# Transposed probabilities of the first two token tiles in another buffer of an encoder kernel

## The chip, the cores and the metric

The kernel runs on one core of one Trainium2 chip. The metric is the device time of one execution in microseconds (us), as the median of several runs. The core has five engines with a queue of instructions each: TensorE (PE, with the weight loads shown apart as PEld), VectorE (DVE), ScalarE (ACT), GpSimd (POOL) and SyncE (SP), whose queue issues most of the transfers (DMA). An engine takes its instructions in the order of its queue; semaphores make it wait for the others.

## The reference

A hybrid encoder trunk of one layer on 1024 tokens with 1024 channels. Three residual sub-layers, each as `x <- LayerNorm(alpha * x + f(x))`: a token mixer (mLSTM heads beside neighbourhood attention), cross-attention from every token into 256 memory tokens, and a gated ConvFFN. The change lies at the seam between the first two. The attention and the sums around it:

```python
def memory_xattn(x, mem, w_q, w_kv, w_o, b_o):
    q = (x @ w_q).reshape(b, t, XA_HEADS, XA_DIM).astype(jnp.float32)
    ...
    s = jnp.einsum('bthd,bmhd->bhtm', q, k) * (XA_DIM ** -0.5)
    p = jax.nn.softmax(s, axis=-1)
    o = jnp.einsum('bhtm,bmhd->bthd', p, v).reshape(b, t, d).astype(x.dtype)
    return o @ w_o + b_o

h = layer_norm(DN_ALPHA * h + hybrid_mixer(...), ln1_w[l], ln1_b[l])
h = layer_norm(DN_ALPHA * h + memory_xattn(h, mem, ...), ln2_w[l], ln2_b[l])
h = layer_norm(DN_ALPHA * h + conv_ffn(h, ...), ln3_w[l], ln3_b[l])
```

## The kernel before, in words

Tokens are worked on in eight tiles of 128. Products are made in half precision with every operand split in a high and a low part, so that one product is three matmuls (`mm3`, lines 223 to 226: high x high on L224, high x low on L225, low x high on L226). These lines are shared by all stages; a row of the profile is told apart by its tiles.

**First norm.** The second half of the mixer's output product runs over the tiles in the order `todo = [0, 2, 1, 3, 4, 6, 5, 7]` (L1313). After each tile `after1` normalizes it (`ln_tile`), multiplies it with `ln1_w` on VectorE (L1305) and adds `ln1_b` on GpSimd (L1306). The two vectors lie in the buffers with the tags `vec0` and `vec1`, the bias `b_xo` in `vec2`. These three buffers are used again and again through the kernel.

**Cross-attention.** Key and value products are folded beforehand with the query and output weights, so that a tile needs two stages:

- `to_hT` (L1266) splits the normalized tile and has SyncE's queue transpose both parts (two DMA transposes, L1271) into `h1T`, of which there are two buffers. `scores(n)` makes 48 matmuls in two halves (`S<-kq,h1T`), takes maxima (L1392), exponentials (L1396), reciprocal sums (L1399), and splits the probabilities into `Ps` (ScalarE L203, VectorE L204).
- `to_PT(n)` has SyncE's queue transpose both parts of `Ps` (two DMA transposes, L1411) into a `vec` buffer: tile n in `vec0` or `vec1` by turns, the last in `vec2`. `out_d(n)` makes 48 matmuls with it (`S<-whi,vec`), adds the residual on VectorE (L1422), takes the second norm and stores the tile.

The loop around them does `scores(n + 1)`, `to_PT(n)`, `to_hT(n + 2)`, `out_d(n - 1)` for each n. `to_B` (L1325) follows `out_d` with a lag of one tile: TensorE transposes the normalized tile; an even tile is kept, an odd one makes the token sums T1 to T4 with its even partner, split in two parts on L1358 and L1359. T2 and T4 lie in the buffer X1h, T1 and T3 in X1l; both buffers are of 4096 float32 a partition and held, until then, the mixer's first half (read by the matmuls `fill`). The sums are operands of the ConvFFN's up-projection, whose weight units `Units.prep` prepares (GpSimd differences from L1521 on, splits on L203 and L204).

**What sets the order.** The program is written in the order above, but line 1927 opens the framework with `schedule_with_timeline_sim=True`: the order of each engine's queue is settled when the kernel is built, from a simulated timeline, with the order of the program as priority. A tile that is allocated in a buffer waits for all readers of the tile that held the buffer before (`reuse_waits="tile"`, L66 to L69). `issue_after` puts single instructions behind others by hand.

Of the kernel before, what the change touches and what calls it, by code (L numbers as in the profile page):

```python
# [8 lines left out]
F32 = mybir.dt.float32  # L9
# [8 lines left out]
D = 1024  # L18
# [38 lines left out]
def encoder(ctx, tc, I, out):  # L57
    nc = tc.nc
    V, A, G, T, S = nc.vector, nc.scalar, nc.gpsimd, nc.tensor, nc.sync
# [7 lines left out]
    vecs = ctx.enter_context(tc.tile_pool(name="vecs", bufs=1, reuse_waits="tile"))  # L67
    wp = ctx.enter_context(tc.tile_pool(name="weights", bufs=1, reuse_waits="tile"))
    xp = ctx.enter_context(tc.tile_pool(name="acts", bufs=1, reuse_waits="tile"))  # L69
# [15 lines left out]
    def tbank():  # L85
        return pp.tile([128, 512], F32, name="tp", tag="tp", bufs=2).rearrange("p (k t) -> p k t", k=4)
# [194 lines left out]
    with ExitStack() as ca:  # L281

        yml = None
        with ExitStack() as cm:
# [258 lines left out]
            with ExitStack() as c2:  # L543
# [12 lines left out]
                with ExitStack() as c1:  # L556
# [162 lines left out]
                T24, T13 = (xp.tile([128, 4096], F32, name="T" + x_, tag=x_).bitcast(F16).rearrange(  # L719
                    "p (n k t) -> p n k t", n=4, k=4) for x_ in ("X1h", "X1l"))  # L720
# [513 lines left out]
    with ExitStack() as cb_:  # L1234
# [3 lines left out]
        f16 = lambda t: t.bitcast(F16)  # L1238

        def evict_wb(q, dst, src, wb, i):  # L1240

            w, b = wb[:, i:i + 1], wb[:, 8 + i:9 + i]
            if q == 0 or i < 6:
                A.activation(dst, src, AF.Identity, scale=w, bias=b)
            else:
                V.tensor_scalar(dst, src, w, b, op0=OP.mult, op1=OP.add)
# [34 lines left out]
        with ExitStack() as cB:  # L1281
# [21 lines left out]
            def after1(tt, r):  # L1303
# [5 lines left out]
                if tt == todo[4]:  # L1309
# [6 lines left out]

        Bh = f16(xp.tile([128, 4096], F32, name="Bh", tag="X2h")).rearrange("p (n q k t) -> p n q k t", n=2, q=2, k=4)
        B1s = xp.tile([128, 4096], F32, name="Bf", tag="X2l").rearrange("p (i q k t) -> p i q k t", i=4, q=2, k=4)
        T24, T13 = (f16(xp.tile([128, 4096], F32, name="T" + t, tag=t)).rearrange("p (n k t) -> p n k t", n=4, k=4)
                    for t in ("X1h", "X1l"))  # L1320
        Bop = {"B11": (Bh[:, 0, 0], Bh[:, 1, 0]), "B21": (Bh[:, 0, 1], Bh[:, 1, 1]),
               "T1": (T13[:, 0], T13[:, 1]), "T3": (T13[:, 2], T13[:, 3]),
               "T2": (T24[:, 0], T24[:, 1]), "T4": (T24[:, 2], T24[:, 3])}

        def to_B(r, tt):  # L1325

            o = slice(tt // 2 * 128, tt // 2 * 128 + 128)
            pts = []
            for q in range(2):
                pt = tbank()  # L1330
                for k in range(4):
                    T.transpose(pt[:, k, :], r[:, (4 * q + k) * 128:(4 * q + k + 1) * 128], ident)
                pts.append(pt)
            B1 = B1s[:, tt // 2]
            spare = lambda i: vecs.tile([128, D], F32, name=f"spare{i}", tag=f"vec{i}")
            if tt % 2:
                if tt == todo[-1]:
                    r = spare(1)
                dst = [r[:, i * 512:i * 512 + 512].rearrange("p (k t) -> p k t", k=4) for i in range(2)]
            else:  # L1340
                dst = [B1[:, q] for q in range(2)]
            for q in range(2):
                for k in range(4):
                    i = 4 * q + k
                    evict_wb(q, dst[q][:, k], pts[q][:, k], wb2, i)
            if tt % 2 == 0:
                for q in range(2):
                    A.activation(Bh[:, 0, q, :, o], B1[:, q], AF.Copy)
                    V.tensor_tensor(Bh[:, 1, q, :, o], B1[:, q], Bh[:, 0, q, :, o], OP.subtract)
                return  # L1350
            e12, e22 = dst
            t12, t34 = ((spare(2 * i) if tt == todo[-1] else
                         wp.tile([128, WP], F32, name="wraw", tag="wraw", bufs=2)[:, :1024]).rearrange(
                "p (i k t) -> p i k t", i=2, k=4) for i in range(2))
            T1, T2, T3, T4 = t12[:, 0], t12[:, 1], t34[:, 0], t34[:, 1]
            def pair(n, src):
                h, l = (t[:, :, o] for t in Bop[n])
                A.activation(h, src, AF.Copy)  # L1358
                (G if n in ("B22", "T3") else V).tensor_tensor(l, src, h, OP.subtract)  # L1359

            V.tensor_tensor(T1, e12, B1[:, 0], OP.subtract)
            V.tensor_tensor(T2, e22, T1, OP.subtract)
            pair("T2", T2)
            pair("T1", T1)
            V.tensor_tensor(T3, e22, e12, OP.subtract)
            pair("B22", e22)
            pair("T3", T3)
            V.tensor_tensor(T4, B1[:, 1], T2, OP.subtract)
            pair("T4", T4)
# [11 lines left out]
        def scores(ck, n):  # L1381
# [21 lines left out]
                    split16(hl[:, 0, o], hl[:, 1, o], P[:, o], mn[:, 4 + h:5 + h])  # L1403
            return hl

        def to_PT(hl, n):
            i = 2 if n == NT - 1 else n % 2
            t = f16(vecs.tile([128, D], F32, name=f"vec{i}", tag=f"vec{i}")).rearrange(
                "p (n k t) -> p n k t", n=2, k=8)
            for i in range(2):  # L1410
                S.dma_start_transpose(t[:, i], hl[:, i])  # L1411
            probs[n] = t

        def out_d(n, lag=1):

            r, t, tt = rs.pop(n), probs.pop(n), todo[n]
            for ch in range(2):
                ps = bank("S2")
                c = slice(ch * 512, ch * 512 + 512)
                for k in range(8):  # L1420
                    mm3(ps, t[:, 0, k], t[:, 1, k], Vo[0][k][:, c], Vo[1][k][:, c], k == 0, k == 7)
                V.scalar_tensor_tensor(r[:, c], r[:, c], alx, ps, op0=OP.mult, op1=OP.add)  # L1422
                yield
            holds.append(ln_tile(r, None, None, small, hold=holds[-1] if holds else None, late=n == NT - 1, eps=epx))
            stores.append(S.dma_start(h2_d[tt * 128:(tt + 1) * 128, :], r))
            rq.append((r, tt))
            if len(rq) > lag:
                to_B(*rq.pop(0))
            yield
# [5 lines left out]
        for n in range(NT - 1):  # L1435
            Pn = scores(ck, n + 1)
            to_PT(P, n)
            P = Pn
            if n + 2 < NT:
                to_hT(ck, n + 2, rs[n + 2])  # L1440
                G.tensor_tensor(rs[n + 2], rs[n + 2], bxo, OP.add)
            if 0 < n < NT - 2:
                run(out_d(n - 1))
        to_PT(P, NT - 1)
        cC.close()

# [109 lines left out]
        next(o6)  # L1556
        next(prep0)
        to_B(*rq.pop(0))
        run(o6)
        run(prep0)  # L1560
# [7 lines left out]
        prep1 = units.prep(1, True)  # L1568
        next(prep1)
        to_B(*rq.pop(0))  # L1570

        with rtx:
# [201 lines left out]
        with ExitStack() as cF:  # L1774
# [13 lines left out]
            for j in range(1, 5):  # L1788
                for tt in range(NT):
# [3 lines left out]
                    if tt in (0, 4) and j < 4:  # L1793
                        f = 4 * j + 4 + tt // 2
# [29 lines left out]
            for tt in range(NT):  # L1824
# [10 lines left out]
                n = 256 if last else 512  # L1835
# [5 lines left out]
                for i in range(2 if last else 1):  # L1841
                    c = slice(i * 512, i * 512 + 512) if last else slice(0, D)
# [88 lines left out]
```

## Time and profile before

| what | us |
|---|---|
| median of 3 runs | 1515.85 (1513.14 to 1516.48) |
| profiled execution, own time | 1512.6 |
| its span, first to last instruction | 1510.5 |
| TensorE busy | 1444.8 (96%) |
| VectorE busy | 1038.1 (69%) |
| ScalarE busy | 824.9 (55%) |
| GpSimd busy | 575.0 (38%) |
| mean granted TensorE clock | 0.988 of full speed |

The profile is of one execution, by the hardware profiler. Times in its rows are from the start of the span, durations in us or, in groups, ns. A row of the timeline reads: start, duration, engine, line of the kernel, operation, tile written <- tiles read, shapes, how many; in square brackets the time that the engine stood idle before, and what it waited for. `SPq` is SyncE's queue of transfers. Matmuls are pipelined, and their ends are modelled: two of them that start 0.22 us apart are each shown with 0.38 us.

### The profile page before, as it was taken

To read this page: it belongs to the slowest core of one execution; us is meant where nothing else is said; L and a number is where in the kernel's file an instruction comes from. 1 tells how busy PE (TensorE), PEld (TensorE's weight loads), DVE (VectorE), ACT (ScalarE), POOL (GpSimd) and SP (SyncE) were. 2 spreads that over 40 slices of the span, in tenths; PEclk is the share of its full clock that TensorE was granted. 3 is DMA by queue.
4 is the path that set the end of the run, shared out by engine and by line. 5 is a ranking of instruction groups with operands and counts; after the bars stand their busy time and mean duration, and the time that the engine had idled before them with its cause. 6 is when DMAs were issued, how large, how long until landed. Compare 5 with 4: busy or idle time off the path is not lost. (4 is left out here: it accounts for less than half of the span.)

```text
span 1510.5 us, 21655 instructions
## 1 busy us (share of the span) xinstructions
PE 1444.8 (96%) x8060; PEld 867.4 (57%) x8060; DVE 1038.1 (69%) x1945; ACT 824.9 (55%) x1393; POOL 575.0 (38%) x453
## 2 busy tenths in 40 slices
PE   8999999999999898997999889999999999999998
PEld 6998776456766787863444434444444444444444
DVE  7867866546677678588455769887787789707424
ACT  5766565655544566424444768777777767503000
POOL 5442357303325765055111464434443420300543
PEclk9999999999999999998999989999999999999999
DMA  8846653325545634743332242223322436713121
GB/s 303 322 159 213 196 187 125 89 53 148 159 119 161 209 119 135 257 126 62 81 77 82 88 153 112 112 112 126 112 112 113 166 112 225 278 41 98 48 79 56
DMA packets 116383, 208.61 MB, mean 138 GB/s; under 512 B 40627, under 2 KB 69555, under 8 KB 112950
## 3 DMA queue, kind: packets, MB, share of 16 engines
q1 hardware_dynamic: 115984, 206.47, 41.3%
q8 instruction: 63, 1.03, 0.3%
q0 software_dynamic: 144, 0.49, 0.2%
q14 instruction: 42, 0.34, 0.1%
q10 hardware_dynamic: 150, 0.27, 0.0%
HBM read 154.15 MB, written 45.15 MB: 132 GB/s over the span
## 5 line engine op out<-in xcount | busy, mean ns | idle before, releaser
L1521 POOL TENSOR_TENSOR wraw<-ur 128x512 f32<-128x512 f32 x22 | 45.7, 2076 | 206.0 <-issue 191.1
L225 PE MATMUL dn<-wlo,yp 128*128 128x512 f16 (+1 forms) x284 | 105.1, 370 | 0.0
L224 PE MATMUL dn<-whi,yp 128*128 128x512 f16 (+1 forms) x284 | 104.9, 370 | 0.0
L226 PE MATMUL dn<-whi,yp 128*128 128x512 f16 (+1 forms) x284 | 104.4, 370 | 0.0
L1609 DVE SCALAR_TENSOR_TENSOR cbuf<-C,wdw,cbuf 128x1024 f32<-128x1024 f32 x44 | 69.6, 1583 | 35.1 <-ACT cbuf L1608 34.9
L226 PEld LDWEIGHTS <-wlo 128*128 128x128 f16 x540 | 52.8, 98 | 57.2 <-DVE wlo L204 1.9
L225 PEld LDWEIGHTS <-whi 128*128 128x128 f16 x540 | 52.8, 98 | 56.0 <-issue 3.2
L224 PEld LDWEIGHTS <-whi 128*128 128x128 f16 x540 | 52.9, 98 | 53.5 <-ACT whi L203 0.6
L242 POOL TENSOR_TENSOR lnrs<-lnrs,mhalf 128x1 f32<-128x1 f32 x32 | 26.0, 812 | 145.9 <-DVE lnrs L241 140.2
L204 DVE SCALAR_TENSOR_TENSOR wlo<-wraw,us,whi 128x1024 f16<-128x1024 f32 (+1 forms) x48 | 62.7, 1323 | 18.7 <-ACT whi L203 18.7
L1610 DVE SCALAR_TENSOR_TENSOR cbuf<-C,wdw,cbuf 128x1024 f32<-128x1024 f32 x44 | 70.2, 1596 | 0.7
L252 ACT ACTIVATE r<-r,lnrs 128x1024 f32<-128x1024 f32 x19 | 23.5, 1239 | 72.3 <-DVE lnrs L251 72.2
L203 ACT ACTIVATE whi<-wraw,us 128x1024 f16<-128x1024 f32 (+1 forms) x48 | 51.2, 1103 | 15.7 <-DVE us L176 14.8
L225 PEld LDWEIGHTS <-yp 128*128 128x128 f16 x370 | 36.2, 98 | 39.9
L224 PEld LDWEIGHTS <-yp 128*128 128x128 f16 x370 | 36.2, 98 | 39.9
L226 PEld LDWEIGHTS <-yp 128*128 128x128 f16 x370 | 36.2, 98 | 39.7
L1608 ACT ACTIVATE cbuf<-C,bdw,wdw 128x1024 f32<-128x1024 f32 x44 | 54.2, 1233 | 8.8 <-DVE C L1646 8.2
L224 PE MATMUL S<-whi,vec 128*128 128x512 f16 x128 | 49.5, 387 | 9.2 <-DMA vec<-Ps 9.2
L224 PE MATMUL tk<-whi,Bo 128*128 128x256 f16 (+1 forms) x192 | 53.3, 277 | 1.6 <-DVE stage L204 1.6
L225 PE MATMUL tk<-wlo,Bo 128*128 128x256 f16 (+1 forms) x192 | 53.4, 278 | 0.0
L226 PE MATMUL tk<-whi,Bo 128*128 128x256 f16 (+1 forms) x192 | 53.3, 278 | 0.0
L225 PE MATMUL tk<-wlo,Be 128*128 128x256 f16 (+1 forms) x192 | 52.4, 274 | 0.9 <-DVE wlo L204 0.9
(520 smaller groups left out, 4898.0 us busy)
## 6 DMA issues: line engine op xcount, KB each, us to landing
ur<-in_w_up_dram SPq DMA_DIRECT2D x22, 1024.0 KB
sv<-in_w_down_dram SPq DMA_DIRECT2D x22, 512.0 KB
y<-cbuf SPq DMA_DIRECT2D x22, 512.0 KB
ur<-y SPq DMA_DIRECT2D x11, 1024.0 KB
wraw<-in_w_down_dram SPq DMA_DIRECT2D x22, 512.0 KB
r<-h SPq DMA_DIRECT2D x11, 512.0 KB
wraw<-in_w_tok_dram SPq DMA_DIRECT2D x10, 512.0 KB
wr<-in_w_xk_dram SPq DMA_DIRECT2D x8, 512.0 KB
```

The costliest lines, as they stand in the source:

```text
L203: A.activation(hi, src, AF.Copy, scale=s)
L204: return V.scalar_tensor_tensor(lo, src, s, hi, op0=OP.mult, op1=OP.subtract)
L224: T.matmul(ps, lh, rh, start=first, stop=False, skip_group_check=skip)
L225: T.matmul(ps, lh, rl, start=False, stop=False, skip_group_check=skip)
L226: return T.matmul(ps, ll, rh, start=False, stop=last, skip_group_check=skip)
L242: G.tensor_tensor(rs[:, 0:1], rs[:, 0:1], mhalf[:, 0:1], OP.pow)
L252: A.activation(r, r, AF.Identity, scale=rs[:, 0:1], bias=rs[:, 1:2])
L1521: G.tensor_tensor(S1, A21, A22, OP.add)
L1608: A.activation(c, C[:, 1:SEQ + 1], AF.Identity, scale=wdw[:, 1, j:j + 1], bias=bdw[:, j:j + 1])
L1609: V.scalar_tensor_tensor(c, C[:, 0:SEQ], wdw[:, 0, j:j + 1], c, op0=OP.mult, op1=OP.add)
L1610: V.scalar_tensor_tensor(c, C[:, 2:SEQ + 2], wdw[:, 2, j:j + 1], c, op0=OP.mult, op1=OP.add)
```

## The change

Two things. The transposed probabilities of the first two tiles (n = 0 and 1) get a home of their own in the buffer X1h, in place of `vec0` and `vec1`; tiles 2 to 7 stay as they were. And the token sums T1 to T4, which lie in X1h and X1l, are allocated only when the first odd tile makes its sums, no longer ahead of the attention.

```diff
-        T24, T13 = (f16(xp.tile([128, 4096], F32, name="T" + t, tag=t)).rearrange("p (n k t) -> p n k t", n=4, k=4)
-                    for t in ("X1h", "X1l"))
-        Bop = {"B11": (Bh[:, 0, 0], Bh[:, 1, 0]), "B21": (Bh[:, 0, 1], Bh[:, 1, 1]),
-               "T1": (T13[:, 0], T13[:, 1]), "T3": (T13[:, 2], T13[:, 3]),
-               "T2": (T24[:, 0], T24[:, 1]), "T4": (T24[:, 2], T24[:, 3])}
+        Bop = {"B11": (Bh[:, 0, 0], Bh[:, 1, 0]), "B21": (Bh[:, 0, 1], Bh[:, 1, 1])}
+
+        def sum_homes():
+            T24, T13 = (f16(xp.tile([128, 4096], F32, name="T" + t, tag=t)).rearrange("p (n k t) -> p n k t", n=4, k=4)
+                        for t in ("X1h", "X1l"))
+            Bop.update({"T1": (T13[:, 0], T13[:, 1]), "T3": (T13[:, 2], T13[:, 3]),
+                        "T2": (T24[:, 0], T24[:, 1]), "T4": (T24[:, 2], T24[:, 3])})
...
                 return
+            if "T1" not in Bop:
+                sum_homes()
             e12, e22 = dst
...
+        early = f16(xp.tile([128, 4096], F32, name="PTe", tag="X1h")).rearrange("p (i c) -> p i c", i=4)
+
         def to_PT(hl, n):
             i = 2 if n == NT - 1 else n % 2
-            t = f16(vecs.tile([128, D], F32, name=f"vec{i}", tag=f"vec{i}")).rearrange(
+            t = (early[:, n] if n < 2 else f16(vecs.tile([128, D], F32, name=f"vec{i}", tag=f"vec{i}"))).rearrange(
                 "p (n k t) -> p n k t", n=2, k=8)
             for i in range(2):
                 S.dma_start_transpose(t[:, i], hl[:, i])
```

## The prediction

> **What bounds the kernel now.** I read the page first, then TensorE's waits between 640 and 870 us, then stretches of busy time, and last the single rows of TensorE, SyncE's queue and VectorE around the one long wait.
>
> ```profile
> span 1510.5 us, 21655 instructions
> PE 1444.8 (96%) x8060; PEld 867.4 (57%) x8060; DVE 1038.1 (69%) x1945; ACT 824.9 (55%) x1393; POOL 575.0 (38%) x453
> ```
> TensorE is busy for 1444.8 of 1510.5 us, so 65.7 us is all that TensorE loses. In the stage that the change touches the waits are these:
>
> ```profile
> PE S L224 <- DMA vec<-Ps: 9.2, 1, 9.2
> PE z L224 <- ACT TX1l L1358: 2.8, 1, 2.8
> ```
> One wait of 9.2 us, once, for a transfer that writes a `vec` tile out of `Ps`: the transposed probabilities of a token tile. The stretches (length, then busy time of each engine with its instructions, granted clock, DMA share, GB/s) show what surrounds it:
>
> ```profile
> 690.00:701.70 11.70, 11.70 (x56) 5.26 (x54) 10.54 (x19) 5.70 (x16) 8.40 (x5) 1.00 0.16 31
> 701.70:711.10 9.40, 0.30 (x2) 0.00 (x0) 8.51 (x10) 3.31 (x7) 4.86 (x2) 0.74 0.21 42
> 711.10:716.50 5.40, 5.35 (x13) 1.94 (x14) 2.95 (x10) 4.10 (x12) 0.00 (x0) 0.50 1.15 164
> 716.50:725.00 8.50, 8.50 (x40) 3.82 (x39) 3.06 (x5) 1.15 (x1) 2.35 (x1) 1.00 0.19 37
> ...
> 825.00:845.00 20.00, 20.00 (x101) 9.92 (x100) 10.17 (x20) 13.42 (x20) 5.54 (x5) 1.00 0.42 146
> ```
> TensorE is full up to 701.7 us and full again from 711 until 845 us (first and last stretches shown; those between are as full); VectorE has room from 711 us on. So TensorE's queue is the path here, and what it loses at 702 us moves everything behind it. The wait costs twice: after it the clock stands at 0.50 for 5.4 us.
>
> **What is waited for.** I call `s0` to `s7` the two score products of a tile (48 matmuls), `PT(n)` the two DMA transposes of tile n's probabilities (L1411; the first makes the high parts, the second the low parts), `out0` to `out7` the 48 matmuls that use them. TensorE's rows:
>
> ```profile
> 701.40 0.38 PE L224 MATMUL S<-kq,h1T 128*128 128x512 f16 x1
> 701.62 0.38 PE L225 MATMUL S<-kq,h1T 128*128 128x512 f16 x1
> 711.15 0.61 PE L224 MATMUL S<-whi,vec 128*128 128x512 f16 x1 [9.15 <-DMA vec<-Ps]
> ...
> 712.83 0.63 PE L226 MATMUL S<-kq,h1T 128*128 128x512 f16 x1
> 713.26 0.63 PE L224 MATMUL S<-kq,h1T 128*128 128x512 f16 x1
> 713.68 0.63 PE L226 MATMUL S<-whi,vec 128*128 128x512 f16 x1
> ...
> 716.59 0.38 PE L224 MATMUL S<-whi,vec 128*128 128x512 f16 x1
> ```
> ```profile
> L224 PE MATMUL S<-kq,h1T x128: 379/379/634, 667.1 to 816.6; 128*128 128x512 f16 x128
> ```
> Scores start at 667.1 us. The 34.5 us to 701.62 us at about 0.216 us a matmul (0.22 in the first two rows) are 160 steps, so 161 matmuls: 3 x 48 for s0 to s2 and 17 of s3. s2 therefore ends at 667.1 + 144 x 0.216 = 698.2 us. Two matmuls of s3 stand in the middle of out0 (712.83, 713.26): the order of the queue was settled ahead, with s3 as filler for the moments in which the plan thought out0 not ready. The plan was too hopeful by 9.15 us. Now SyncE's queue, which issues the transposes, and VectorE:
>
> ```profile
> L1411 SPq EVENT_SEMAPHORE  x15: 17/28/16541, 690.7 to 823.9; - x15
> ```
> ```profile
> 677.67 12.97 SPq L1271 DMA_TRANSPOSE h1T<-h1s  x4
> 707.92 2.60 SPq L1411 DMA_TRANSPOSE vec<-Ps  x2
> 710.70 1.25 SPq L1271 DMA_TRANSPOSE h1T<-h1s  x1
> 712.05 3.43 SPq L1411 DMA_TRANSPOSE vec<-Ps  x2
> ```
> ```profile
> 694.57 1.65 DVE L204 SCALAR_TENSOR_TENSOR Ps<-P,mn,Ps 128x256 f16<-128x256 f32 x2
> ...
> 704.85 3.05 DVE L1305 TENSOR_TENSOR r<-r,vec 128x1024 f32<-128x1024 f32 x1
> 707.82 2.95 DVE L204 SCALAR_TENSOR_TENSOR Ps<-P,mn,Ps 128x256 f16<-128x256 f32 x2
> ```
> SyncE stands at L1411 from 690.7 us and issues PT(0) at 707.92 us. The last split of tile 0's probabilities (694.57 + 1.65) was over at 696.22 us; the last of tile 1's follow only at 707.82 us. What ends at 704.85 + 3.05 = 707.90 us is the last multiplication with `ln1_w` (L1305), which reads vec0, the tile that PT(0) overwrites. The wait of 690.7 to 707.9 us thus has two parts: the data until 696.2 us, the place until 707.9 us. First matmul after issue: 711.15 - 707.92 = 3.23 us.
>
> **The change, part by part.**
>
> PT(0) and PT(1) go to X1h. Its last readers before:
>
> ```profile
> L225 PE MATMUL fill<-wlo,X1h x64: 387/389/398, 471.9 to 594.7; 128*128 128x512 f32 x64
> ```
> They ended 100 us earlier, so the place is free. Nothing is added: the same 16 transposes from the same queue, no arithmetic. PT(0) issues when its data are there, 696.22 us instead of 707.92, and its high part lands at 696.22 + 3.23 = 699.45 us, the low part 1.3 us later (half of the 2.60 us of the pair). TensorE reaches out0 at 698.2 us if the plan now puts it right behind s2, or at 701.8 us if it stays behind 17 matmuls of s3. In the first case 1.25 us of waiting is left (the low part is first needed by the seventh matmul, 1.3 us on, as in the rows above: no wait of its own); in the second none.
>
> Restart: from 711.15 to 716.59 us stand 13 matmuls; at 0.216 us they are 2.81 us, so 2.63 us went to the half clock. A rest of 1.25 us should keep the clock; the rows nearest to it:
>
> ```profile
> 865.00:885.00 20.00, 13.72 (x52) 5.57 (x52) 18.66 (x21) 12.31 (x16) 16.62 (x23) 0.74 0.37 132
> 885.00:905.00 20.00, 19.17 (x91) 8.64 (x89) 8.66 (x13) 12.48 (x17) 10.38 (x8) 1.00 0.43 157
> ```
> With 0.83 us idle the clock is 1.00, with 6.28 us idle it is 0.74. The Trainium skill (TensorE: Matmul & The Clock Gate, Part 1: The HAM clock gate) says that an idle window of about 3.4 us halves the clock and about 3.4 us of work restores it. The trace agrees with the halving; its 5.4 us at 0.50 is longer than the page's window, by which the restart would be worth 1.7 us, not 2.63, and the gain 0.9 us less.
>
> Upper end of the gain: 9.15 + 2.63 = 11.8 us. I take the nearer plan, out0 right behind s2, since PT(0) becomes ready earlier in any plan: 11.8 - 1.3 = 10.5 us.
>
> PT(2) and PT(3) become the first to write vec0 and vec1 and no longer wait for out0 and out1. TensorE doesn't wait for them now (it is full from 716.5 us), so nothing comes of it.
>
> The homes of the token sums are allocated at the first odd tile's sums instead of ahead of the stage. That issues nothing; the writes of X1h now need out0 and out1 to be over:
>
> ```profile
> L1358 ACT ACTIVATE TX1h<-wraw x6: 622/630/631, 789.8 to 861.2; 128x512 f16<-128x512 f32 x6
> ```
> The first write is at 789.8 us; out1 is over near 741 us (716.6 us, then the 37 matmuls left of out0, 29 of s3 and 48 of out1 at 0.216 us), so the cover is over 40 us. Without it ScalarE would stand at L1358.
>
> What is late next: out1, which needs PT(1). TensorE now does s2, out0, s3, out1: out0 ends at 699.45 + 10.4 (48 x 0.216) = 709.8, s3 at 720.2 us. PT(1), issued at 712.05 us, lands at 715.3 and 716.6 us. But VectorE gets out0's sums earlier, perhaps ahead of the splits of tile 1:
>
> ```profile
> 721.23 0.74 DVE L1422 SCALAR_TENSOR_TENSOR r<-r,sc,S 128x512 f32<-128x512 f32 x1
> 722.00 0.69 DVE L237 BATCH_NORM_STATS2 lnst<-r 128x6 f32<-128x512 f32 x1
> ```
> ```profile
> 721.45 2.35 POOL L1441 TENSOR_TENSOR r<-r,vec 128x1024 f32<-128x1024 f32 x1 [10.96 <-DVE h1s L204]
> ```
> Two of each are 2.9 us: PT(1) then lands at 719.5 us, still before 720.2. That price should hold while GpSimd works, as it does around 705 us: these two VectorE rows ran beside a GpSimd addition (721.45 to 723.8 us).
>
> The gain carries: TensorE is full until 845 us, and the chain of waits behind it starts from the last scores:
>
> ```profile
> 816.50 0.56 ACT P L1396 x2
> ```
> The work behind that point hangs on it and on TensorE, so I let it move as one. The sum: the profiled execution took 1512.6 us (2.1 us around its span), 1512.6 - 10.5 = 1502.1; it lay 3.25 us below the median of the three runs, 1515.85 us, and from that the forecast is 1505.4 us.
>
> **The rivals.**
>
> *The queue takes the wait over.* SyncE works in order. In the rows above the transposes of tile 4's input (710.70) stand behind PT(0). If the new plan put them ahead, they would go when s2 has freed their slot, 698.2 us, take 2.6 us, and PT(0)'s high part would land at 700.8 + 3.2 = 704.0 us. TensorE would idle for 2.2 us (from 701.8) or 5.8 us with a restart (8.4 us): 11.8 less that is a gain of 9.6 or 3.4 us, 1506.3 to 1512.5 us. Against it: PT(0) becomes ready earlier, not later, and was ahead already.
>
> *The wait moves to PT(1).* If the plan puts out1 straight behind out0, TensorE reaches it at 709.8 us, PT(1) lands at 715.3 us, or 718.2 with VectorE's extra 2.9 us. Idle 5.5 to 8.4 and a restart of 2.6 us take 8.1 to 11.0 us of 10.5: 1513.5 to 1516.4 us, no change. This is also the case in which the change moves a wait and does nothing else. For it: the plan was 9 us too hopeful about PT(0), and VectorE has 8.51 of 9.40 us filled there. Against it: s3 is ready and comes first in the program.
>
> *Slower: the last tile's token sums fall behind unit preparation.* The order of every engine is planned anew. TensorE idles 6.28 us in 865 to 885 us, part of it for token sums (TX1l in the waits above); VectorE has 18.66 us and GpSimd 16.62 of 20 filled there. If the last tile's sums are queued behind the four differences of the next unit and three splits:
>
> ```profile
> L1521 POOL TENSOR_TENSOR wraw<-ur 128x512 f32<-128x512 f32 x22 | 45.7, 2076 | 206.0 <-issue 191.1
> ...
> L204 DVE SCALAR_TENSOR_TENSOR wlo<-wraw,us,whi 128x1024 f16<-128x1024 f32 (+1 forms) x48 | 62.7, 1323 | 18.7 <-ACT whi L203 18.7
> ```
> 4 x 2.08 + 3 x 1.32 = 12.3 us more idle and another 2.6 us of half clock make 14.9 us; against 10.5 that is 4.4 slower, 1520.3 us. It decides from 10.5 us of extra idle at that place. Against it: sums, unit loads and preparation all start from the same last scores and move together.
>
> **How the numbers follow.** Forecast 0.66; the queue 0.12; the wait at PT(1) 0.10; slower 0.12. A measurement of this kernel can tell about 0.2% (3 us: 1512.8 to 1518.9 us) from no change. Faster: 0.66 + 0.12 = 0.78; within: 0.10; slower: 0.12. The range goes up to the end of the second rival, 1516.4 us. Down: the full 11.8 us give 1504.1; the three runs spread 1.7 us to either side; a new plan could save the other half-clock restart too, 2.6 us: 1499.8 us. Outside are the slower case and a few in a hundred below.
>
> **What would show it.** Right: no wait of TensorE on `Ps` transposes over 1.5 us, the first such transpose issued near 696 us, the clock at 1.00 between 700 and 720 us, out0 starting by 702 us, last scores about 10.5 us earlier than 817, and the tail shifted alike. Wrong: a wait of 5 us or more at the second pair, L1271 transposes ahead of the first pair, or a stretch from last scores to the end that is longer than now.

## The result, and the profile after

| | before | after |
|---|---|---|
| median, us | 1515.69 (1513.14 to 1516.58, 6 runs) | 1503.22 (1502.08 to 1506.29, 6 runs) |
| profiled execution: own time, span | 1512.6, 1510.5 | 1502.1, 1500.0 |
| TensorE busy, us | 1444.8 | 1441.3 |

The changed kernel is faster: ratio 0.9924, 95% interval 0.9911 to 0.9937, that is 12.5 us by the medians and 9.5 to 13.5 us by the interval. The forecast was 1505.4 us.

In the profile after, lines of the kernel behind L1323 stand 2 to 6 further down (the transposes of probabilities are L1417 now). TensorE's waits between 640 and 870 us:

```profile
PE z L225 <- DVE TX1l L1363: 3.7, 1, 3.7
PE z L224 <- ACT TX1l L1362: 2.9, 1, 2.9
PE z L224 <- ACT TX1h L1362: 1.1, 1, 1.1
PE mx L182 <- ACT spare L1244: 0.8, 1, 0.8
PE S L226 <- DMA PTe<-Ps: 0.7, 1, 0.7
```
The wait of 9.2 us is gone; what is left of it is the last row, 0.7 us, now for a tile PTe (in X1h) and on L226, the first matmul that needs the low part. The stretches that correspond to those of before:

```profile
690.00:701.70 11.70, 11.00 (x52) 4.84 (x51) 10.00 (x21) 6.01 (x14) 7.21 (x5) 1.00 0.60 91
701.70:711.10 9.40, 9.40 (x46) 4.23 (x44) 7.05 (x11) 4.28 (x10) 4.70 (x2) 1.00 0.51 97
711.10:716.50 5.40, 5.40 (x27) 2.45 (x26) 4.13 (x9) 3.17 (x8) 0.25 (x1) 1.00 0.43 82
716.50:725.00 8.50, 8.50 (x41) 3.90 (x40) 5.06 (x14) 3.27 (x8) 2.66 (x2) 1.00 0.60 136
```
TensorE is full where it had 0.30 us in 9.40, and the granted clock is 1.00 where it was 0.74 and 0.50: 27 matmuls in 711.1 to 716.5 us, not 13. TensorE's rows at the seam:

```profile
696.83 0.38 PE L226 MATMUL S<-kq,h1T 128*128 128x512 f16 x1
697.05 0.38 PE L224 MATMUL S<-whi,PTe 128*128 128x512 f16 x1
697.26 0.38 PE L225 MATMUL S<-wlo,PTe 128*128 128x512 f16 x1
698.34 0.39 PE L226 MATMUL S<-whi,PTe 128*128 128x512 f16 x1 [0.70 <-DMA PTe<-Ps]
```
out0 follows s2 without a gap (696.83, 697.05), and waits once, for the low part. SyncE's queue of transposes and the split that it waits for, on ScalarE (high) and VectorE (low):

```profile
676.56 2.61 SPq L1271 DMA_TRANSPOSE h1T<-h1s  x2
693.08 3.22 SPq L1417 DMA_TRANSPOSE PTe<-Ps  x2
696.39 2.66 SPq L1271 DMA_TRANSPOSE h1T<-h1s  x2
702.99 4.80 SPq L1417 DMA_TRANSPOSE PTe<-Ps  x2
707.89 2.64 SPq L1271 DMA_TRANSPOSE h1T<-h1s  x2
```
```profile
692.14 0.91 ACT L203 ACTIVATE Ps<-P,mn 128x256 f16<-128x256 f32 x2 [2.60 <-DVE mn L1404]
```
```profile
693.38 1.66 DVE L204 SCALAR_TENSOR_TENSOR Ps<-P,mn,Ps 128x256 f16<-128x256 f32 x2
```
The high transpose issues at 693.08 us, 0.03 us after ScalarE's high split (692.14 + 0.91); the low one can follow when VectorE's split ends at 695.04 us. Nothing but the data holds PT(0) any more. PT(1) issues at 702.99 us, where it was 712.05.

Where the time came from is read best from the first score matmul of the attention to its last, a stretch that holds the same 658 matmuls in both kernels and in which TensorE never stops but at this seam:

```profile
L224 PE MATMUL S<-kq,h1T x128: 379/379/389, 666.0 to 804.4; 128*128 128x512 f16 x128
...
L226 PE MATMUL S<-kq,h1T x128: 379/379/379, 666.4 to 804.8; 128*128 128x512 f16 x128
```
Before, the rows of the same two lines say 667.1 to 816.6 (L224) and this:

```profile
L226 PE MATMUL S<-kq,h1T x128: 379/379/634, 667.5 to 817.0; 128*128 128x512 f16 x128
```
From first to last: 149.9 us before (667.1 to 817.0), 138.8 us after (666.0 to 804.8). That is 11.1 us, and the sum of the prediction gives it: 9.15 of idling plus 2.63 of half clock, less the 0.70 us that is left, is 11.08. Outside the stretch the two executions differ by no more than repeats do: 1.1 us up to the first score, 1.7 us the other way from the last score to the end (693.5 and 695.2 us). The changed kernel profiled once more has its first score 1.4 us later, at 667.4 us, and a last part of 694.3 us; in the eleven executions profiled for the experiments this last part lies between 693.0 and 696.8 us. So single spans don't settle a microsecond; below, the stretch does.

### The profile page after: what moved, and what is told of

Its sections match the earlier page's. It is cut to its first block, busy times and chain, and to the rows that moved or that the text cites. A ratio compares the mean times of both kernels' runs of the same rounds, so it can differ in the third digit from the quotient of the medians.

```text
span 1500.0 us, 21659 instructions
## 1 busy us (share of the span) xinstructions
PE 1441.3 (96%) x8060; PEld 867.1 (58%) x8060; DVE 1036.0 (69%) x1945; ACT 825.7 (55%) x1393; POOL 575.1 (38%) x453
## 5 line engine op out<-in xcount | busy, mean ns | idle before, releaser
L224 PE MATMUL dn<-whi,yp 128*128 128x512 f16 (+1 forms) x284 | 104.9, 370 | 0.0
L226 PE MATMUL dn<-whi,yp 128*128 128x512 f16 (+1 forms) x284 | 104.4, 370 | 0.0
L226 PEld LDWEIGHTS <-wlo 128*128 128x128 f16 x540 | 52.8, 98 | 56.5 <-DVE wlo L204 1.3
L224 PEld LDWEIGHTS <-whi 128*128 128x128 f16 x540 | 52.8, 98 | 53.1 <-ACT whi L203 0.3
L242 POOL TENSOR_TENSOR lnrs<-lnrs,mhalf 128x1 f32<-128x1 f32 x32 | 25.9, 809 | 137.9 <-DVE lnrs L241 132.2
L224 PEld LDWEIGHTS <-yp 128*128 128x128 f16 x370 | 36.2, 98 | 39.8
L226 PEld LDWEIGHTS <-yp 128*128 128x128 f16 x370 | 36.2, 98 | 39.7
L224 PE MATMUL tk<-whi,Bo 128*128 128x256 f16 (+1 forms) x192 | 52.6, 274 | 2.5 <-DVE stage L204 2.5
L224 PE MATMUL tk<-whi,Be 128*128 128x256 f16 (+1 forms) x192 | 52.6, 274 | 0.7 <-DVE stage L204 0.7
L226 PE MATMUL tk<-whi,Be 128*128 128x256 f16 (+1 forms) x192 | 52.5, 274 | 0.0
```

The source lines that it names most:

```text
L224: T.matmul(ps, lh, rh, start=first, stop=False, skip_group_check=skip)
L226: return T.matmul(ps, ll, rh, start=False, stop=last, skip_group_check=skip)
L242: G.tensor_tensor(rs[:, 0:1], rs[:, 0:1], mhalf[:, 0:1], OP.pow)
```

## The experiments

The theory: TensorE waited for PT(0)'s place, vec0, and for the restart that followed; nothing else in the change matters. The rivals: the freed places of other tiles, the later allocation and the new plan of the queues, or a price of the restart that isn't real. Ratios are to the kernel before, run beside each (medians of 1514.8 to 1515.0 us in the rounds of the experiments); "stretch" is first to last score matmul, of the one profiled execution of each kernel. It holds 657 or 658 matmuls in every kernel but the two with filler.

| kernel | median, us | ratio (95% interval) | stretch, us |
|---|---|---|---|
| before | 1515.69 | 1 | 149.9 |
| after | 1503.22 | 0.9924 (0.9911 to 0.9937) | 138.8 |
| tile 0 only in X1h | 1503.77 | 0.9922 (0.9908 to 0.9937) | 138.9 |
| tile 1 only in X1h | 1514.52 | 0.9995 (0.9984 to 1.0006) | 150.1 |
| token sums later, no more | 1514.38 | 1.0003 (0.9991 to 1.0015) | 149.8 |
| norm vectors in X1h | 1500.46 | 0.9908 (0.9890 to 0.9925) | 138.8 |
| tiles 0 to 3 in X1h | 1503.29 | 0.9916 (0.9902 to 0.9929) | 138.9 |
| busy filler | 1510.37 | 0.9967 (0.9954 to 0.9979) | 142.7 |
| busy filler, pinned | 1508.76 | 0.9960 (0.9947 to 0.9972) | 147.2 |
| out1 ahead of s3 | 1505.59 | 0.9938 (0.9924 to 0.9951) | 141.0 |
| low parts last | 1502.85 | 0.9917 (0.9903 to 0.9930) | 137.9 |
| vectors in X1h, low parts last | 1499.99 | 0.9894 (0.9878 to 0.9909) | 138.0 |
| after, once more | 1502.87 | 0.9916 (0.9903 to 0.9930) | 138.8 |

**Which part does it.** Tile 0 alone:

```diff
-            t = (early[:, n] if n < 2 else f16(vecs.tile(...))).rearrange(
+            t = (early[:, n] if n < 1 else f16(vecs.tile(...))).rearrange(
```


> Only tile 0's transposes go to X1h; tile 1's stay in vec1. Theory (the gain is tile 0's wait for its place): as the changed kernel, 1503 us within 2; first to last score matmul about 139 us (138.8 in the changed kernel, 149.9 in the one before); tile 1's transposes wait for the last addition of ln1_b, near 709 us, land near 713 and are not waited for. Rival (both tiles are needed, or the wait moves to tile 1): a wait of 5 us or more at the second pair of transposes, 1510 us or more.

It gave 1503.77 us and 138.9 us. Its second pair of transposes, into vec1, shows what tile 1's place costs; the queue and the last addition of `ln1_b` on GpSimd:

```profile
709.88 2.61 SPq L1417 DMA_TRANSPOSE vec<-Ps  x2
```
```profile
707.51 2.34 POOL L1306 TENSOR_TENSOR r<-r,vec 128x1024 f32<-128x1024 f32 x1 [4.32 <-DVE r L1305]
```
It issues 0.03 us after that addition (709.85 us), and TensorE doesn't notice: out1 comes only behind s3. Tile 1 alone (`n == 1` in the same place):

> Only tile 1's transposes go to X1h; tile 0's stay in vec0. Theory: as the kernel before, 1515.7 us within 2, with one wait of about 9 us and a stretch of about 150 us from first to last score matmul. Rival (tile 1, the later allocation or the new order give part of the gain): 1512 us or less.

1514.52 us, and TensorE's wait is there:

```profile
PE S L224 <- DMA vec<-Ps: 9.0, 1, 9.0
```
The later allocation alone (the kernel before, with the token sums' tiles allocated at the first odd tile and all transposes in the `vec` buffers):

> Only the later allocation of the token sums; all transposes where they were. Theory: as the kernel before, 1515.7 us within 2, the wait of 9.2 us still there. Rival (the allocation and the order that follows from it carry part of the gain): 1512 us or less.

1514.38 us, the wait at 9.2 us, the interval around 1. Allocation and the plan that follows from it carry nothing that this interval (1.4 us down, 2.3 us up) would show; they only make X1h free to use.

**The place, from its other side.** The vectors go to X1h, tiles 0 and 1 keep vec0 and vec1:

```diff
-            lw, lb = vec(0, "ln1_w"), vec(1, "ln1_b")
+            lwb = xp.tile([128, 4096], F32, name="lwb", tag="X1h").rearrange("p (i c) -> p i c", i=4)
+            lw, lb = lwb[:, 0], lwb[:, 1]
+            S.dma_start(lw, bcast_row(I["ln1_w"], D))
+            S.dma_start(lb, bcast_row(I["ln1_b"], D))
...
-            t = (early[:, n] if n < 2 else f16(vecs.tile(...))).rearrange(
+            t = f16(vecs.tile(...)).rearrange(
```


> The other side is moved: the first norm's two vectors are loaded into X1h, tiles 0 and 1 keep vec0 and vec1, and tiles 2 and 3 again have to wait for the products of tiles 0 and 1. Theory: as the changed kernel, 1503 us within 2, stretch of about 139 us, no wait of TensorE on transposes over 1.5 us. Rival (the freed places of tiles 2 and 3, or X1h itself, matter): a part of the 12 us is missing, 1506 us or more.

The same wait goes in another way, with the same stretch of 138.8 us and the same 0.7 us left:

```profile
PE S L226 <- DMA vec<-Ps: 0.7, 1, 0.7
```
Here tiles 2 and 3 again write behind tiles 0 and 1; that costs nothing in the stretch. The time, 1500.46 us, misses the expected 1503 within 2 by 0.5 us on the fast side; more on that below. The opposite, tiles 0 to 3 in X1h (`n < 4`):

> The transposes of tiles 0 to 3 go to X1h, so that tiles 2 to 5 also have a free place. Theory: nothing waits on those places, 1503 us within 2 and a stretch of about 139 us. Rival (freed places matter): 1501 us or less. Other side (the token sums now wait for tile 3's product before they may write X1h): 1505 us or more.

1503.29 us and 138.9 us: more free places bring nothing, and TensorE's waits for the token sums stay (2.9, 1.3 and 3.7 us). Freed places of later tiles are out as a cause.

**Idle or busy.** 43 matmuls whose result nobody reads, between the scores of tile 2 and out0:

```diff
+            if n == 1:
+                junk = tbank().rearrange("p k t -> p (k t)")
+                for _ in range(43):
+                    T.matmul(junk, Kq[0][:, 0, :128], Kq[0][:, 0, :512], start=True, stop=True)
             if 0 < n < NT - 2:
                 run(out_d(n - 1))
```


> The changed kernel with 43 idle-filling matmuls, whose result nobody reads, ahead of tile 0's product: TensorE loses 43 x 0.216 = 9.3 us there, about the 9.15 us that it idled before, but stays busy. Theory (TensorE is the path, and the old wait also cost 2.6 us of half clock): the changed kernel plus 9.3 less the 0.7 us of wait that the filler covers, 1511.8 us, stretch 147.4 us, so 3 to 4 us faster than the kernel before. Rival (the half clock costs nothing of the end): as the kernel before, 1515.7 us and 149.9 us. Second rival (TensorE is not the path): less than 6 us slower than the changed kernel.

1510.37 us is near the 1511.8 expected, but the stretch is 142.7 us, not 147.4: the plan used 21 of the 43 earlier, from 639.1 us on.

```profile
L1451 PE MATMUL tp<-kq x43: 379/379/379, 639.1 to 706.5; 128*128 128x512 f16 x43
```
So it doesn't compare like with like, and was repeated with the filler tied behind s2 (`tc.issue_after` on its last matmul):

> The filler again, its 43 matmuls now queued behind the last score matmul of tile 2, so that all of them stand where the kernel before idled (in the first try the plan used part of them earlier, from 639 us on). Theory (TensorE is the path, and the old wait cost 9.15 us of idling and 2.6 us of half clock): stretch from first to last score matmul 138.8 + 9.3 - 0.7 = 147.4 us against 149.9 before, time 8.6 us over the changed kernel. Rival (the half clock costs the end nothing): 149.9 us.

Now the filler stands in one piece where the idling was (row of its line, then the stretch of its place), and the clock holds:

```profile
L1452 PE MATMUL tp<-kq x43: 379/379/379, 700.1 to 709.1; 128*128 128x512 f16 x43
```
```profile
699.70:709.20 9.50, 9.50 (x46) 4.32 (x45) 7.35 (x13) 5.08 (x10) 4.89 (x3) 1.00 0.73 104
```
The stretch is 147.2 us (669.0 to 816.2): 8.4 us over the changed kernel, against 8.6 expected, and 2.7 us under the kernel before. 9.3 us of useless work cost TensorE less than 9.15 us of idling, by the half clock; the stretches of the kernels with the long wait (149.8 to 150.1 us) and of those with 0.7 or 0.8 us in its place (138.8 to 138.9) vary far less than that. The time agrees in direction alone. It lies 5.9 us over the changed kernel run beside it, not 8.6 (the intervals of the two ratios leave that open between some 3 and 10 us), and 4.2 to 8.0 us under the kernel before, where the stretch has 2.7: at least 1.5 us of that lies outside the stretch and isn't explained.

**The second rival's price.** out1 straight behind out0, ahead of s3:

```diff
-            if 0 < n < NT - 2:
+            if 0 < n < NT - 2 and n != 2:
                 run(out_d(n - 1))
+            if n == 1:
+                run(out_d(1))
```


> The product of tile 1 stands straight behind that of tile 0, ahead of the scores of tile 3. By the prediction's price of the second rival TensorE would wait 5.5 to 8.4 us for tile 1's transposes and lose 8.1 to 11.0 us: 1511 to 1514 us. By the trace of the changed kernel those transposes are issued at 702.99 us, 9 us earlier than the prediction had it, so they land near 706 and 710 us and TensorE, there at 707.6 us, waits 2.2 us at most: 1503 to 1506 us.

1505.59 us, stretch 141.0: 2.2 us lost, 1.8 of them in the last two of these waits of TensorE:

```profile
701.48 0.39 PE L226 MATMUL S<-whi,PTe 128*128 128x512 f16 x1 [0.72 <-DMA PTe<-Ps]
713.32 0.39 PE L226 MATMUL S<-whi,PTe 128*128 128x512 f16 x1 [1.31 <-DMA PTe<-Ps]
723.91 1.09 PE L1334 MATMUL tp<-ident,r 128*128 128x128 f32 x8 [0.49 <-ACT r L252]
```
The first is the 0.7 us of the changed kernel; 1.31 us is the wait for tile 1's low part, and in the 0.49 us TensorE's transposes of a normalized tile wait for its norm. The price of 8.1 to 11.0 us in the prediction was wrong.

**The rest of 0.7 us.** In tile 0's product the matmuls with the low part go to the end of each half:

```diff
-                for k in range(8):
-                    mm3(ps, t[:, 0, k], t[:, 1, k], Vo[0][k][:, c], Vo[1][k][:, c], k == 0, k == 7)
+                if n == 0:
+                    for k in range(8):
+                        T.matmul(ps, t[:, 0, k], Vo[0][k][:, c], start=k == 0, stop=False)
+                        T.matmul(ps, t[:, 0, k], Vo[1][k][:, c], start=False, stop=False)
+                    for k in range(8):
+                        T.matmul(ps, t[:, 1, k], Vo[0][k][:, c], start=False, stop=k == 7)
+                else:
...
```


> The changed kernel, with the matmuls of tile 0's product that use the low part of the probabilities at the end of each half. Theory: the remaining wait of 0.7 us for the low transposes goes, first to last score matmul 138.1 us, 1502.5 us, not to be told from the changed kernel by its time. Rival (TensorE is held there by something else): the wait stays or moves to another tile.

The wait is gone and the stretch is 137.9 us; 1502.85 us is the same as the changed kernel by time. Together with the vectors in X1h:

> Both at once: the first norm's vectors in X1h instead of the transposes, and the low parts last in tile 0's product. Theory: stretch 138.0 us, time within 2 us of the changed kernel run beside it, since the place of the vectors gave the same stretch. Rival (moving the vectors is better by itself, as its median of 1500.5 us hinted): 2 us or more below the changed kernel.

> The changed kernel as it is, beside the other two for comparison: 12 us below the kernel before, stretch 138.8 us.

Side by side 1499.99 and 1502.87 us, with 138.0 and 138.8 us of stretch. The stretch explains 0.8 of the 2.9 us. The 2.9 us are more than the 2 us of the theory, and by the medians the rival's bound is met. Both kernels with the vectors in X1h (1500.46 and 1499.99 us) lie under all with the transposes there, but the intervals touch (0.9878 to 0.9909 and 0.9903 to 0.9930), and the profiled executions (1501.93 and 1502.5 us) show no place for the other 2 us: that stays open. The combination has the lowest median of this study.

## Why the prediction was right

**The cause** was right, and the experiments isolate it: the wait from 696 to 708 us was for vec0. With tile 0's place free the gain is whole, without it there is none, and a free vec0 in place of X1h does the same.

**The sum.** 9.15 + 2.63 us stood as predicted; the filler bears out the 2.63 (2.7 us between a busy and an idle pause). The rest left behind was put at 1.25 us and is 0.70. The step that was off is "PT(0) issues when its data are there, 696.22 us": that took both splits together. The high transpose needs ScalarE's half alone and issued at 693.08 us, 694.2 on the clock of the execution before; it landed before s2 was through. The low one issued behind VectorE's half at 695.04 us, and TensorE took it up at 698.34, 3.3 us later. The prediction also had the remaining wait on the wrong half. It put the 1.25 us on the high part and none on the low one, since that is "first needed by the seventh matmul"; but the queue that it read this from has two matmuls of s3 and two more with high parts in between. Behind s2 the low part is needed by the third matmul, and there the 0.70 us lies. With the prediction's own issue time that would have left 2.1 us: its two errors pull apart, and that 1.25 us came near the 0.70 is in part luck. So 11.1 us by the profile in place of 10.5, against 12.5 us (9.5 to 13.5) measured.

That the profiled execution took 1502.1 us, just the 1512.6 - 10.5 of the prediction, is luck as well: 11.1 us in the stretch and 1.1 before it, less 1.7 behind it. The 1505.4 us of the forecast add the 3.25 us by which one profiled execution lay under its median; after the change that distance was 1.1 us. This, and not the mechanism, is most of the 2.2 us between forecast and median.

**The plan.** out0 went straight behind s2, as taken. Two things of the queue were not foreseen. PT(0) now stands ahead of the transposes of tile 3's input, which wait behind it until 696.39 us (before they were through at 690.6). That costs nothing, since they are through at 699.05 us and s3 begins only 9 us later. And "PT(1), issued at 712.05 us" was carried over as if it were a time of its data; it was a time of its place and queue. It stood behind the last addition of `ln1_b`, 710.5 us, and a transpose of tile 4's input; the row of the addition before, and of tile 1's last high split on ScalarE:

```profile
707.98 2.51 POOL L1306 TENSOR_TENSOR r<-r,vec 128x1024 f32<-128x1024 f32 x1 [1.16 <-DVE r L1305]
```
```profile
704.04 0.90 ACT L203 ACTIVATE Ps<-P,mn 128x256 f16<-128x256 f32 x2
```
Its high data were there at 704.94 us. Its low data came at 710.77 us before and come at 706.53 us now (703.94 + 2.59, the same split on VectorE), behind the last multiplication with `ln1_w`, which starts at 702.20 us where it was 704.85. The same step that the prediction made for tile 0 (data or place?) was left out for tile 1; hence the price of the second rival, 8.1 to 11.0 us, which the run puts at 2.2.

**The cover.** VectorE's sums of out0 did not come ahead of tile 1's splits: its first L1428 row starts at 714.16 us, behind them. The first write of token sums into X1h is at 777.6 us, 12.2 us earlier like everything there. The slower case did not come: token sums after the last scores wait as before (2.9, 1.1 and 3.7 us, where it was 2.8, 1.3 and 3.7), and the part after the last score, 1.7 us longer than before, lies within what repeats show. The prediction's sign of being wrong, a longer part behind the last scores, can't tell so small a difference.

## What to carry to other kernels

A transfer's wait has a part for its data and a part for the place that it overwrites; ask for both, for every tile that shares the place, and for each half of the tile by itself. If the data are there well before the place, and some large buffer lies idle at that moment, borrowing it can cost nothing, as here, provided its next owner is allocated later. Before pricing a rival by the time at which something happened, ask what held it at that time, for the change may take that away too.

## What the runs showed of the hardware

A pause of TensorE cost more idle than busy. After 9.15 us without work the clock stood at 0.50 for 5.4 us, which cost 2.6 us; with 9.3 us of useless matmuls in the same place it stayed at 1.00. The pauses of 0.70 us in the changed kernel and 1.31 us in the kernel with out1 ahead were followed by matmuls 0.22 us apart, at full speed. The halving agrees with the Trainium skill (TensorE: Matmul & The Clock Gate, Part 1: The HAM clock gate), by which an idle window of about 3.4 us halves the clock, but the return took longer here than the 3.4 us that it names.

Neither the limit nor the return is one fixed number. At the token sums behind the last scores a shorter pause was enough in the changed kernel:

```profile
851.01 0.22 PE L182 MATMUL mx<-identb,am 128*128 128x128 bf16 x1 [0.78 <-ACT spare L1244]
854.08 0.58 PE L224 MATMUL z<-TX1l,unitYh 128*128 128x512 f16 x1 [2.85 <-ACT TX1l L1362]
```
Behind 2.85 us of idling, with one short matmul and another 0.78 us of idling ahead of it, the matmul is shown with 0.58 us and the clock at 0.50. When the same kernel was profiled once more, the matmul behind the same 2.85 us was shown with 0.38 us, at full speed. From the first matmul behind the longest pause there (3.67 us) it took 3.8 us to full speed in the changed kernel and 4.6 us in the kernel before; behind the wait for tile 0 it took 5.1 us with the token sums later alone and 5.9 us with tile 1 alone in X1h. So the 2.63 us of the prediction is the price of one execution. And the 6.28 us of idling that it sets beside a clock of 0.74 is no single rest: it is the sum of three pauses, 1.3 us of one of 2.83 us, 1.32 us and 3.67 us.
